# Sums of the down projection's weights made in both token blocks, with weights fetched a slice ahead, and final norms by pairs of tiles

## The chip, the cores and the metric

The kernel runs on one core of a Trainium2 chip. The metric is the device time of one execution in microseconds (us). Inside the core, TensorE (PE) multiplies; VectorE (DVE), ScalarE (ACT) and GpSimd (POOL) do the elementwise work; SyncE (SP) and POOL issue most of the DMAs. Each engine works through its own instructions strictly in order, and waits on semaphores for the others.

## What is computed

One layer of an encoder on 2048 tokens of width 1024: a token mixer, then a SwiGLU feed-forward network with an inner width of 2816, then a last RMS norm. Cut to the part that the change touches:

```python
x = x + mix                                      # the mixer's result
h = rms_norm(x, norm2[l])
gate, up = jnp.split(h @ w_ffn_in[l], 2, axis=-1)
x = x + (jax.nn.silu(gate) * up) @ w_ffn_out[l]  # w_ffn_out: 2816 x 1024
return rms_norm(x, final_norm)
```

All data is float32, and the results have to keep nearly that precision.

## The kernel before

**Products.** Every operand of a matmul is split into a high part, which TensorE multiplies at its fast rate, and a low remainder. A product is three matmuls, high by high, low by high and high by low (`mm3`, L206 to L209 of the profile). Both halves of the feed-forward network use the Strassen-Winograd scheme: seven products of sums of blocks in place of eight products of blocks.

**Stages.** The mixer works on four blocks of 512 tokens (0 to about 757 us). Then the gate stage (class `Gate`) goes over two blocks of 1024 tokens, block 0 until about 1180 us and block 1 until about 1660 us. In each it takes 22 steps j, one for each pair of 128-wide slices of the inner width; a step has seven products of 12 matmuls 128x512, so 84 matmuls. The products' results are kept (`kept`, ACT copy L895), joined by additions on DVE (L910 to L921) and activated on ACT (L911, L922). The sums of the finished slices are made by `Gate.sums` (L949 to L972) and stored to `ad`. The feed for the following step fetches its weights (`in_wgu_dram`, SP's queue), adds them (L720 to L747) and splits them into high (ACT L217) and low (DVE L218). Last comes the stage `Down`: five groups of inner slices times eight pairs of token tiles; its fifth group also has four plain products, and after it the pair's two tiles get the final norm and are stored.

**Side work in the gate stage.** `spread` takes a list of Python generators and the number of steps of each, and hangs single steps evenly between the products of steps j0 to j1. The list is planned separately for each block:
- In block 0 it holds what block 1 needs at its start: `nb.normed` (20 steps at j 3 to 10) and `nb.differences` (24 steps, from j 12 on).
- In block 1 it holds `w2_sums(k)` for the eleven slice pairs k, at j 2 to 19. A `w2_sums` fetches four raw pieces of 128x512 of `w_ffn_out` (`in_w_dram`, L223, POOL's queue) in its first step. In seven more it forms the seven sums (DVE L995 to L1008) and calls `put` for each: ACT casts the high part (L982), DVE subtracts for the low part (L983), POOL stores both to `w2c` in memory (L985). One k, `PLAIN`, has four puts without sums. In all that is 44 loads, 74 puts and 148 stores. `Down` reads the parts back from `w2c`.

**Buffers and order.** All these buffers come from two arenas, A (float32 work, tile `arena`) and R (matmul operands, tile `arena_r`), with 140 and 264 grains of 128 columns. A freed piece is given out again, and the instruction that writes it first then waits for the last one that read it, a store among them. The engines' order is made by a scheduler from the program's order, not written by hand.

**Final norm.** `finish(s, i)` (called between the products of the next pair, in `run_all`) makes the reciprocal root for one tile by `rsqrt`: 12 instructions on 128x1 data (L195 to L204), then two scalings of 128x512 (L1170) and two stores. `Down.step` adds each product's result from its PSUM bank to the accumulator on DVE (L1101); a bank can be written again only after that.

Of the kernel before, what the change touches and what calls it, by code (L numbers as in the profile page):

```python
# [37 lines left out]
A_GRAINS = 140  # L38
R_GRAINS = 264
# [115 lines left out]
def hybrid_layer_kernel(  # L155
# [37 lines left out]
    def rsqrt(dst, ss, scale, n):  # L193
# [272 lines left out]

    def run(gen, n=None):
        while n is None or n > 0:
            if next(gen, run) is run:
                return  # L470
            if n is not None:
                n -= 1
# [502 lines left out]
    def w2_sums(k):  # L975

        raw = [load(w2[k, n][:, i * T : (i + 1) * T], T, queue=nc.gpsimd) for i in range(2) for n in range(2)]
        b11, b12, b21, b22 = raw

        def put(m, b):  # L980
# [6 lines left out]

        yield
        if k == PLAIN:
            for m, b in enumerate(raw):  # L990
                put(m, b)
                yield
            return
        t1 = A.alloc(T)
        nc.vector.tensor_sub(t1.f(), b12.f(), b11.f())  # L995
        put(0, b11)
        yield
        t2 = A.alloc(T)
        nc.vector.tensor_sub(t2.f(), b22.f(), t1.f())
        put(1, t1)  # L1000
        yield
        nc.vector.tensor_sub(b12.f(), b22.f(), b12.f())
        put(4, b12)
        yield
        put(6, b22)
        yield
        t4 = A.alloc(T)
        nc.vector.tensor_sub(t4.f(), b21.f(), t2.f())  # L1008
        put(2, t2)
        yield  # L1010
        put(3, b21)
        yield
        put(5, t4)
        yield


    class Down:
# [55 lines left out]
        def step(self, at):  # L1073
# [68 lines left out]
            if last:  # L1142
                self.finish(s, 0)
# [7 lines left out]
            if last:  # L1151
                self.finish(s, 1)
# [4 lines left out]
        def squares(self, s, i, n):  # L1157

            if (s, i) not in self.ss:
                self.ss[s, i] = [small(1, "ssf") for _ in range(2)]  # L1160
            sumsq(self.ss[s, i][n], self.acc[s][i].f(2, T)[:, n, :], T)
# [166 lines left out]
```

## Time and profile before

| what | us |
|---|---|
| median of 3 runs | 2112.72 (2112.57 to 2117.39) |
| the profiled execution, its time | 2109.95 |
| its span, first to last instruction | 2107.9 |
| TensorE busy in the span | 2021.6 (96%) |
| gate stage, block 0 | about 757 to 1180 |
| gate stage, block 1; its stretch with the weights' sums | about 1180 to 1660; 1222 to 1605 |
| Down; its last group | 1660 to 2098; 1980 to 2098 |

The page gives busy time for each engine over the whole span. A view of stretches gives the same for each stage, with the count of instructions; a view of waits says which instruction of an engine stood idle, and what released it. TensorE's busy time counts a matmul from its start to its modelled end, and matmuls overlap, so that a stretch full of matmuls at half rate still reads as busy; the count of matmuls in a stretch tells it apart.

### The profile page before, as it was taken

Reading aid. Unit: us, or ns where it says so; the run is one execution under the profiler, and the core shown is the slowest. Engines: PE = TensorE matmul, PEld = TensorE weight load, DVE = VectorE, ACT = ScalarE, POOL = GpSimd, SP = SyncE. Lnnn points to the kernel's source line nnn. Section 1 sums busy time; section 2 is a strip of 40 time slices with the busy share of each in tenths; the row PEclk is TensorE's granted clock in tenths of the full one; section 3 lists DMA queues with packets and bytes.
Section 4 is the critical chain, followed back from the end, with each engine's and each line's share of the span. In section 5 each row is a group of like instructions: output and inputs, shape, how many; then the busy total and the mean of one; then the engine's idle time right before and its main releaser. Section 6 shows DMA issues by size and latency. Waiting matters only on the chain.

```text
span 2107.9 us, 26734 instructions
## 1 busy us (share of the span) xinstructions
PE 2021.6 (96%) x9520; PEld 1656.0 (79%) x9520; DVE 1346.9 (64%) x2474; ACT 885.6 (42%) x1523; POOL 202.9 (10%) x260
## 2 busy tenths in 40 slices
PE   7999999999999999999999999998999999999997
PEld 6788778878878878788888777776777788888776
DVE  6575555464655776565766876766775556565687
ACT  5655545734654553433333644443443212111232
POOL 0000000000000000000000022222221222222110
PEclk9999999999999999999999999999999999999999
DMA  4132245245424634544653766666665955755632
GB/s 170 58 129 75 99 139 197 67 152 174 156 89 141 223 128 125 169 141 140 185 170 114 221 200 220 233 235 195 223 225 177 389 157 190 241 165 165 216 127 80
DMA packets 208359, 353.22 MB, mean 168 GB/s; under 512 B 19409, under 2 KB 95458, under 8 KB 208226
## 3 DMA queue, kind: packets, MB, share of 16 engines
q1 hardware_dynamic: 190562, 292.79, 42.8%
q0 software_dynamic: 17664, 58.73, 7.9%
q8 instruction: 74, 1.21, 0.2%
q14 instruction: 59, 0.48, 0.1%
HBM read 244.49 MB, written 106.95 MB: 167 GB/s over the span
## 4 chain that ended last, share of the span: by engine, by line
PE 64%; DMA 10%; DVE 10%; issue 9%; ACT 4%; POOL 3%; SPq 0%; POOLq 0%; DVEq 0%; ACTq 0%
PE mm L207 21%; PE mm L208 20%; PE mm L209 20%; DVE arena_r L218 2%; DMA w2c<-arena 2%; POOL w2c L985 2%; DMA arena<-in_wgu_dram 2%; DMA ad<-arena 1%; ACT arena_r L217 1%; DVE arena L1101 1%; DMA arena<-in_wf_dram 1%; DVE arena L460 1%; DMA arena_r<-w2c 1%; PE mm L794 1%; DVE arena_r L1068 1%
## 5 line engine op out<-in xcount | busy, mean ns | idle before, releaser
L207 PE MATMUL mm<-arena_r 128*128 128x512 f32 (+1 forms) x2848 | 1114.0, 392 | 48.9 <-ACT arena L895 20.8
L208 PE MATMUL mm<-arena_r 128*128 128x512 f32 (+1 forms) x2848 | 1105.1, 388 | 11.1 <-DVE arena_r L218 7.0
L209 PE MATMUL mm<-arena_r 128*128 128x512 f32 (+1 forms) x2848 | 1098.9, 388 | 6.2 <-DVE arena_r L218 6.2
L207 PEld LDWEIGHTS mm<-arena_r 128*128 128x128 f32 x2848 | 538.5, 189 | 184.5 <-ACT arena L895 35.6
L217 ACT CAST arena_r<-arena 128x512 fp32r<-128x512 f32 (+1 forms) x638 | 376.8, 610 | 626.3 <-PE mm L208 299.2
L209 PEld LDWEIGHTS mm<-arena_r 128*128 128x128 f32 x2848 | 539.4, 190 | 118.0 <-DVE arena_r L218 9.1
L208 PEld LDWEIGHTS mm<-arena_r 128*128 128x128 f32 x2848 | 540.2, 190 | 116.6 <-DVE arena_r L218 14.0
L218 DVE TENSOR_TENSOR arena_r<-arena,arena_r 128x512 fp32r<-128x512 f32 (+1 forms) x638 | 411.7, 674 | 263.2 <-ACT arena_r L217 194.7
L1101 DVE TENSOR_TENSOR arena<-arena,mm 128x512 f32<-128x512 f32 x288 | 197.4, 687 | 139.0 <-PE mm L209 138.8
L1067 ACT CAST arena_r<-arena_r 128x896 fp32r<-128x896 f32 (+1 forms) x88 | 80.5, 915 | 302.4 <-PE mm L208 174.0
L1068 POOL TENSOR_TENSOR arena_r<-arena_r 128x896 fp32r<-128x896 f32 x40 | 85.0, 2125 | 323.4 <-PE mm L209 178.0
L985 POOL DMA_DIRECT2D w2c<-arena x148 | 80.1, 543 | 188.1 <-ACT arena L982 154.8
L190 ACT ACTIVATE arena<-arena 128x512 bf16<-128x512 f32 (+1 forms) x80 | 57.0, 713 | 83.8 <-DVE arena L1101 42.8
L223 POOL DMA_DIRECT2D arena<-in_w_dram x44 | 23.8, 542 | 675.1 <-DMA arena<-in_wgu_dram 573.9
L895 ACT COPY arena<-mm 128x512 f32<-128x512 f32 x132 | 76.5, 580 | 9.4 <-PE mm L209 9.4
L982 ACT CAST arena<-arena 128x512 fp32r<-128x512 f32 x74 | 45.6, 620 | 79.7 <-DMA arena<-in_w_dram 24.0
L918 DVE TENSOR_TENSOR arena<-mm,arena 128x512 f32<-128x512 f32 x44 | 30.3, 688 | 41.9 <-PE mm L209 41.9
L1068 DVE TENSOR_TENSOR arena_r<-arena_r 128x896 fp32r<-128x896 f32 (+1 forms) x48 | 50.1, 1044 | 9.8 <-ACT arena_r L1067 9.2
L983 DVE TENSOR_TENSOR arena<-arena 128x512 fp32r<-128x512 f32 x74 | 49.6, 687 | 9.2 <-ACT arena L982 8.4
L910 DVE TENSOR_TENSOR arena<-mm,arena 128x512 f32<-128x512 f32 x44 | 30.3, 688 | 39.2 <-PE mm L209 39.2
L616 POOL COPY stc<-arena 128x256 f32<-128x256 f32 x4 | 3.6, 904 | 473.6 <-ACT arena L190 134.2
L921 DVE TENSOR_TENSOR arena<-mm,arena 128x512 f32<-128x512 f32 x44 | 30.3, 689 | 28.0 <-PE mm L209 28.0
(133 smaller groups left out, 1113.7 us busy)
## 6 DMA issues: line engine op xcount, KB each, us to landing
arena<-in_wgu_dram SPq DMA_DIRECT2D x176, 256.0 KB, 3.6
ad<-arena SPq DMA_DIRECT2D x148, 256.0 KB, 3.4
w2c<-arena POOLq DMA_DIRECT2D x148, 256.0 KB, 3.7
arena_r<-w2c SPq DMA_DIRECT2D x148, 256.0 KB, 5.6
arena_r<-ad SPq DMA_DIRECT2D x80, 448.0 KB, 3.6
arena<-in_wf_dram SPq DMA_DIRECT2D x40, 512.0 KB, 3.6
arena<-in_wo_dram SPq DMA_DIRECT2D x32, 512.0 KB, 3.7
arena<-in_w_dram POOLq DMA_DIRECT2D x44, 256.0 KB, 4.4
```

The source lines that it names most:

```text
L190: nc.scalar.activation(b.ap.bitcast(BF16), src, AF.Square, accum_out=dst)
L207: nc.tensor.matmul(ps, lhsT=sh, rhs=mh, start=first, stop=False, skip_group_check=again)
L208: nc.tensor.matmul(ps, lhsT=sh, rhs=ml, start=False, stop=False, skip_group_check=again)
L209: nc.tensor.matmul(ps, lhsT=sl, rhs=mh, start=False, stop=last, skip_group_check=again)
L217: nc.scalar.copy(hi, src)
L218: nc.vector.tensor_sub(lo, src, hi.bitcast(F32))
L895: nc.scalar.copy(b.f(), ps[:, :n])
L983: nc.vector.tensor_sub(b.f().bitcast(F32R), b.f(), hi.f())
L985: nc.gpsimd.dma_start(w2c[k][:, m, i * T : (i + 1) * T], part.f())
L1067: nc.scalar.copy(hi, v)
L1068: (nc.gpsimd if i == 1 else nc.vector).tensor_tensor(lo, v, hi.bitcast(F32), op=ALU.subtract)
L1101: nc.vector.tensor_add(c, c, ps)
```

## The change

- `w2_sums` becomes one generator for all eleven k. It fetches the four raw pieces of the next k right after the fifth of seven puts of a k (for `PLAIN` after the third of four), before the last two puts. The sums themselves and `put` stay.
- This one generator is hung into both gate blocks: 30 of its 75 steps in block 0 at j 12 to 19, 45 in block 1 at j 2 to 19. To make room, `normed` moves from j 3 to 10 to j 3 to 7, and `differences` from j 12 on to j 8 to 11.
- Arena A gets 144 grains, R 260.
- `rsqrt` becomes a generator of parts. `finish` takes a pair's two tiles at once, with the 12 small instructions on 128x2 data for both, and one part of it is run before each further product of the next pair. The last pair is still done by single tiles.

```diff
-A_GRAINS = 140
-R_GRAINS = 264
+A_GRAINS = 144
+R_GRAINS = 260
...
-    def rsqrt(dst, ss, scale, n):
+    def rsqrt_parts(dst, ss, scale, n):
...
+            if it != 1:
+                yield
+
+    def rsqrt(*args):
+        run(rsqrt_parts(*args))
...
-    def w2_sums(k):
-
-        raw = [load(w2[k, n][:, i * T : (i + 1) * T], T, queue=nc.gpsimd) for i in range(2) for n in range(2)]
-        b11, b12, b21, b22 = raw
-
-        def put(m, b):
+    def w2_sums(ks):
+
+        raws = {}
+
+        def fetch(i):
+            if i < len(ks):
+                k = ks[i]
+                raws[i] = [load(w2[k, n][:, h * T : (h + 1) * T], T, queue=nc.gpsimd)
+                           for h in range(2) for n in range(2)]
+
+        def put(k, m, b):
...
+        fetch(0)
         yield
...
+            t4 = A.alloc(T)
+            nc.vector.tensor_sub(t4.f(), b21.f(), t2.f())
+            put(k, 2, t2)
+            fetch(i + 1)
+            yield
+            put(k, 3, b21)
+            yield
+            put(k, 5, t4)
+            yield
...
-        def finish(self, s, i):
-
-            rs = small(1, "rsf")
-            rsqrt(rs, self.ss.pop((s, i)), 1.0 / D, 1)
-            b, t = self.acc[s][i], self.tiles(s)[i]
...
+        def finish(self, s, which=(0, 1)):
+
+            m = len(which)
+            rs = small(m, "rsf")
+            i0 = which[0]
+            yield from rsqrt_parts(rs, [v[:, i0 : i0 + m] for v in self.ss[s]], 1.0 / D, m)
+            for i in which:
+                b, t = self.acc[s][i], self.tiles(s)[i]
+                for n in (1, 0):
...
+                    yield
+                A.free(b)
...
-                    if ks == len(self.groups) - 1 and r in (2, 4) and s > 0:
-                        self.finish(s - 1, r // 2 - 1)
+                    if r:
+                        run(done, 1)
                 run(nxt)
+                run(done)
+                if ks == len(self.groups) - 1:
+                    done = self.finish(s)
...
+    w2_side = w2_sums(range(NJ // 2))
...
-            spread([nb.normed(hf) for hf in range(2)], [KC + 2] * 2, 3, 11)
-            spread([nb.differences(c) for c in range(4)], [6] * 4, 12, NJ - 3)
+            spread([nb.normed(hf) for hf in range(2)], [KC + 2] * 2, 3, 8)
+            spread([nb.differences(c) for c in range(4)], [6] * 4, 8, 12)
+            spread([w2_side], [30], 12, NJ - 2)
         else:
-            spread([w2_sums(k) for k in range(NJ // 2)], [8] * (NJ // 2), 2, NJ - 2)
+            spread([w2_side], [45], 2, NJ - 2)
```

The changed program has as many instructions on TensorE, ACT, SP and POOL as before; on DVE it has 84 fewer. Its lines are numbered anew: L223 is L235, L982, L983 and L985 are L992, L993 and L995, L895 is L900, L217 is L229, L1101 is L1118, L1170 is L1190, and L195 to L204 are L202 to L211.

On POOL's queue, before, from the middle of the sums in block 1: `in_w_dram` is a raw weight piece that is fetched, `w2c` a part that is stored, and POOL takes no other work there.

```order
L223 DMA arena<-in_w_dram 128x512 x3
L985 DMA w2c<-arena 128x512 x13
L223 DMA arena<-in_w_dram 128x512 x2
L985 DMA w2c<-arena 128x512
L223 DMA arena<-in_w_dram 128x512 x2
L985 DMA w2c<-arena 128x512 x10
L223 DMA arena<-in_w_dram 128x512 x3
```

On POOL's queue, after, the end of block 0's part and the start of block 1's; `x2d` pieces are accumulators of `Down`'s first pairs.

```order
L235 DMA arena<-in_w_dram 128x512 x3
L995 DMA w2c<-arena 128x512 x13
L235 DMA arena<-in_w_dram 128x512 x2
L995 DMA w2c<-arena 128x512
L235 DMA arena<-in_w_dram 128x512 x2
L995 DMA w2c<-arena 128x512 x7
L235 DMA arena<-x2d_70 128x1024
L235 DMA arena<-x2d_74 128x1024
L995 DMA w2c<-arena 128x512 x3
L235 DMA arena<-in_w_dram 128x512
```

The queue's pattern stays, loads with stores between them, since a load can go only into a piece that is free; what moved is its place against the matmuls, and the two `x2d` loads, which stood ahead of all sums.

On DVE, before, the last group of `Down`, near its end: the small instructions of one tile's norm among the additions.

```order
L1101 TENSOR_TENSOR arena<-arena,mm 128x512
L202 SCALAR_TENSOR_TENSOR rt<-ry 128x1
L203 TENSOR_TENSOR rt<-rt,rv 128x1
L204 SCALAR_TENSOR_TENSOR rsf<-rt,ry 128x1
L195 TENSOR_SCALAR rv<-ssf 128x1
L1170 SCALAR_TENSOR_TENSOR arena<-arena,rsf 128x512
L1101 TENSOR_TENSOR arena<-arena,mm 128x512
L1170 SCALAR_TENSOR_TENSOR arena<-arena,rsf 128x512
L197 SCALAR_TENSOR_TENSOR rv<-ssf,rv 128x1
L199 TENSOR_SCALAR ry<-rv 128x1
L202 SCALAR_TENSOR_TENSOR rt<-ry 128x1
L203 TENSOR_TENSOR rt<-rt,rv 128x1
```

On DVE, after, at the same place, with the norm of a pair of tiles.

```order
L1118 TENSOR_TENSOR arena<-arena,mm 128x512
L210 TENSOR_TENSOR rt<-rt,rv 128x2
L211 SCALAR_TENSOR_TENSOR rsf<-rt,ry 128x2
L1190 SCALAR_TENSOR_TENSOR arena<-arena,rsf 128x512 x3
L1118 TENSOR_TENSOR arena<-arena,mm 128x512
L1190 SCALAR_TENSOR_TENSOR arena<-arena,rsf 128x512
L1118 TENSOR_TENSOR arena<-arena,mm 128x512 x5
L202 TENSOR_SCALAR rv<-ssf 128x2
L204 SCALAR_TENSOR_TENSOR rv<-ssf,rv 128x2
L206 TENSOR_SCALAR ry<-rv 128x2
L209 SCALAR_TENSOR_TENSOR rt<-ry 128x2
```

The small instructions come once for a pair, and five additions follow each other without any; three of the pair's four scalings stand together ahead of an addition.

## Rows read from the trace of the kernel before

**Rows 1.** The page: busy time, share of the span and instructions of each engine.

```profile
PE 2021.6 (96%) x9520; PEld 1656.0 (79%) x9520; DVE 1346.9 (64%) x2474; ACT 885.6 (42%) x1523; POOL 202.9 (10%) x260
```

**Rows 2.** Stretches: from:to, length, busy (count) of PE, PEld, DVE, ACT, POOL; clock, DMA share, GB/s.

```profile
757.00:1004.00 247.00, 243.11 (x1094) 198.47 (x1093) 153.20 (x252) 101.94 (x177) 0.00 (x0) 1.00 0.43 137
1004.00:1160.00 156.00, 155.90 (x683) 127.35 (x683) 103.62 (x166) 58.07 (x100) 0.00 (x0) 1.00 0.53 160
...
1222.00:1605.00 383.00, 353.57 (x1494) 282.81 (x1492) 272.74 (x436) 163.11 (x285) 101.58 (x188) 0.98 0.68 224
...
1660.00:1672.00 12.00, 8.72 (x32) 6.48 (x31) 6.72 (x8) 1.82 (x4) 3.67 (x4) 0.86 1.04 355
1672.00:1980.00 308.00, 308.00 (x1358) 254.52 (x1357) 184.02 (x257) 61.94 (x67) 68.57 (x33) 1.00 0.62 205
1980.00:2098.00 118.00, 111.56 (x475) 87.56 (x474) 95.17 (x273) 35.74 (x80) 12.75 (x6) 1.00 0.31 104
```

**Rows 3.** TensorE's waits, 1222 to 1605 us: us in total, times, longest.

```profile
PE mm L207 <- ACT arena L895: 17.3, 13, 3.8
PE mm L207 <- DVE arena L915: 7.0, 3, 3.3
```

**Rows 4.** ACT's waits for DMAs, 1222 to 1605 us.

```profile
ACT arena L982 <- DMA arena<-in_w_dram: 24.0, 9, 6.4
ACT arena L982 <- DMA w2c<-arena: 21.6, 9, 4.2
...
ACT arena L982 <- DMA ad<-arena: 8.4, 4, 3.2
```

**Rows 5.** DVE's waits for DMAs, 1222 to 1605 us.

```profile
DVE arena L995 <- DMA arena<-in_w_dram: 19.2, 6, 6.1
...
DVE arena L956 <- DMA w2c<-arena: 7.6, 5, 2.9
...
DVE arena L965 <- DMA w2c<-arena: 4.2, 2, 2.5
```

**Rows 6.** Timeline around 1507 us: start, length, instruction, idle before and its releaser.

```profile
1506.75 0.54 POOL L223 DMA_DIRECT2D arena<-in_w_dram  x1 [4.90 <-DMA w2c<-arena]
...
1510.22 0.69 DVE L995 TENSOR_TENSOR arena<-arena 128x512 f32<-128x512 f32 x1 [6.09 <-DMA arena<-in_w_dram]
1510.30 1.79 ACT L982 CAST arena<-arena 128x512 fp32r<-128x512 f32 x3 [5.07 <-DMA arena<-in_w_dram]
1510.83 0.68 DVE L915 TENSOR_TENSOR arena<-mm,arena 128x512 f32<-128x512 f32 x1
...
1511.57 0.80 PE L207 MATMUL mm<-arena_r 128*128 128x512 f32 x1 [3.28 <-DVE arena L915]
...
1512.16 0.63 PE L208 MATMUL mm<-arena_r 128*128 128x512 f32 x1
...
1512.59 0.63 PE L209 MATMUL mm<-arena_r 128*128 128x512 f32 x1
```

**Rows 7.** DMA issues, 1222 to 1605 us: KB each, median us to landing.

```profile
w2c<-arena POOLq DMA_DIRECT2D x148, 256.0 KB, 3.7
...
arena<-in_w_dram POOLq DMA_DIRECT2D x40, 256.0 KB, 4.9
```

**Rows 8.** TensorE's waits, block 0, 757 to 1160 us.

```profile
PE mm L207 <- ACT arena L895: 2.3, 3, 1.3
```

**Rows 9.** DVE by line and shape, 1980 to 2108 us: count, busy, mean ns, idle before.

```profile
L1101 DVE TENSOR_TENSOR arena<-arena,mm 128x512 f32<-128x512 f32 x59 | 40.1, 684 | 12.1 <-PE mm L209 11.9
L1170 DVE SCALAR_TENSOR_TENSOR arena<-arena,rsf 128x512 f32<-128x512 f32 x32 | 22.9, 749 | 0.3
...
L203 DVE TENSOR_TENSOR rt<-rt,rv 128x1 f32<-128x1 f32 x48 | 7.6, 158 | 1.4
```

**Rows 10.** DVE by line and shape, whole span: the small product two wide.

```profile
L203 DVE TENSOR_TENSOR rt<-rt,rv 128x2 f32<-128x2 f32 x6 | 0.9, 156 | 0.1
```

**Rows 11.** TensorE's waits, 1980 to 2098 us.

```profile
PE mm L207 <- DVE arena L1101: 6.1, 8, 1.2
```

More of the change, by code (lines that the diff above doesn't have):

```diff
@@ L191, in sumsq, with run @@
         A.free(b)
-    def rsqrt(dst, ss, scale, n):
+    def run(gen, n=None):
+        while n is None or n > 0:
+            if next(gen, run) is run:
+                return
+            if n is not None:
+                n -= 1
+    def rsqrt_parts(dst, ss, scale, n):
         v = small(n, "rv")
@@ L465, in lru_scan @@
         return mb
[L467 to L472, printed above, removed]
     class OutProj:
@@ L986, in put @@
             A.free(hi, b)
+        fetch(0)
         yield
[L989 to L1014, printed above, removed]
+        for i, k in enumerate(ks):
+            raw = raws.pop(i)
+            b11, b12, b21, b22 = raw
+            if k == PLAIN:
+                for m, b in enumerate(raw):
+                    put(k, m, b)
+                    if m == 2:
+                        fetch(i + 1)
+                    yield
+                continue
+            t1 = A.alloc(T)
+            nc.vector.tensor_sub(t1.f(), b12.f(), b11.f())
+            put(k, 0, b11)
+            yield
+            t2 = A.alloc(T)
+            nc.vector.tensor_sub(t2.f(), b22.f(), t1.f())
+            put(k, 1, t1)
+            yield
+            nc.vector.tensor_sub(b12.f(), b22.f(), b12.f())
+            put(k, 4, b12)
+            yield
+            put(k, 6, b22)
+            yield
+            t4 = A.alloc(T)
+            nc.vector.tensor_sub(t4.f(), b21.f(), t2.f())
+            put(k, 2, t2)
+            fetch(i + 1)
+            yield
+            put(k, 3, b21)
+            yield
+            put(k, 5, t4)
+            yield
     class Down:
@@ L1142, in step @@
             if last:
-                self.finish(s, 0)
+                run(self.finish(s, (0,)))
             add(c22, pd)
@@ L1151, in step @@
             if last:
[L1152 removed]
+                run(self.finish(s, (1,)))
                 for m in range(4):
@@ L1157, in squares @@
         def squares(self, s, i, n):
-            if (s, i) not in self.ss:
-                self.ss[s, i] = [small(1, "ssf") for _ in range(2)]
-            sumsq(self.ss[s, i][n], self.acc[s][i].f(2, T)[:, n, :], T)
-        def finish(self, s, i):
-            rs = small(1, "rsf")
-            rsqrt(rs, self.ss.pop((s, i)), 1.0 / D, 1)
-            b, t = self.acc[s][i], self.tiles(s)[i]
-            for n in (1, 0):
-                v = b.f(2, T)[:, n, :]
-                nc.vector.scalar_tensor_tensor(v, v, rs, self.fn.f(2, T)[:, n, :], op0=ALU.mult, op1=ALU.mult)
-                nc.sync.dma_start(out_v[t][:, n * T : (n + 1) * T], v)
-            A.free(b)
+            if s not in self.ss:
+                self.ss[s] = [small(2, "ssf") for _ in range(2)]
+            sumsq(self.ss[s][n][:, i : i + 1], self.acc[s][i].f(2, T)[:, n, :], T)
+        def finish(self, s, which=(0, 1)):
[6 more added lines that the diff above has]
+                for n in (1, 0):
+                    v = b.f(2, T)[:, n, :]
+                    nc.vector.scalar_tensor_tensor(v, v, rs[:, which.index(i) : which.index(i) + 1],
+                                                   self.fn.f(2, T)[:, n, :], op0=ALU.mult, op1=ALU.mult)
+                    nc.sync.dma_start(out_v[t][:, n * T : (n + 1) * T], v)
+                    yield
+                A.free(b)
         def run_all(self, ready):
```

## The prediction

> **What bounds the kernel now.** I read the page first: TensorE is busy for 96% of the span [rows 1], so only two things can shorten the program, fewer matmuls or fewer stretches in which matmuls come late. The change has the same matmuls. So the second view is the one of stretches, and what the reader is to see there is length against count. From 1672 to 1980 us TensorE never idles at full clock: 1358 matmuls in 308 us, 0.2268 us each [rows 2]. I take this as the full rate and ask what the other stretches lose by it. Block 1's stretch with the weights' sums has 1494 matmuls, which need 338.8 us and take 383: it loses 44 us. The last group has 475, 107.7 us, and takes 118: it loses 10. The entry to Down, 1660 to 1672 us, has 32, 7.3 us, and takes 12: it loses nearly 5. Block 0 idles for 3.9 us in its first stretch and 0.1 us in its second [rows 2]; nothing can be won there, but something lost. Behind the last matmul stand about 10 us of norms and stores (2098 to the span's end at 2107.9).
>
> In the sums' stretch the idle time alone is 383 - 353.6 = 29.4 us. The other 15 us are in the busy part: behind a wait of 3.28 us at 1511.57 matmuls start 0.43 us apart (1512.16, 1512.59) [rows 6], and the mean granted clock of the stretch is 0.98 against 1.00 [rows 2]; 0.43 is about twice 0.2268, the lower of the clock's two levels. So a long wait costs its length and some more behind it. The Trainium skill, Perfetto Trace Analysis, section Identifying the Most-Contended Engine, says that busy time of pipelined matmuls is a poor measure, and to look at the share of weight loads. That share is 282.81/383 = 0.738 here and 254.52/308 = 0.826 at full rate [rows 2], so by the rule the stretch loses 383 x (1 - 0.738/0.826) = 41 us; by idle time, 29; a forecast made in proportion to the rule's figure would lie 1 to 2 us above mine.
>
> Who makes TensorE wait there? It waits mostly for the ACT copy L895 (17.3 us) and the DVE addition L915 (7.0 us) [rows 3], the instructions that empty a PSUM bank. They are not slow. They stand in order behind an ACT cast L982 or a DVE subtraction L995 of the weights' sums, which waits for a DMA. Rows 6 show one such chain: a raw load is issued at 1506.75, after POOL had waited 4.90 us for a store to give the buffer free; DVE L995 and ACT L982 wait for its data until 1510.2 and 1510.3; L915 runs at 1510.83 right behind L995; TensorE starts at 1511.57. ACT and DVE together wait there 24.0 + 19.2 = 43.2 us for raw loads, and 21.6 + 8.4 + 7.6 + 4.2 = 41.8 us for stores that still hold a buffer, of the sums or of the gate's results [rows 4, 5].
>
> **The change part by part.** A, the weights' sums. No instruction of them is saved: 44 loads, 74 puts, 148 stores. Three things move. First, a raw load was issued in the step before its first use; now two puts earlier. By the order and its waits the gap between the point at which a load's buffer is free and its first use was 1 to 24 matmuls in the old program (18 or fewer for seven of the eleven k), that is 0.2 to 5.4 us at 0.2268, under or near the median landing of 4.9 us [rows 7]. In the new one it is 18 to 144 for all but the first k (4 to 33 us), nearly all above 4.9 us. So the waits for loads should go. Secondly, the sums go over 8 + 18 = 26 steps j in place of 18, so all waits thin out by 18/26, if they come by crowding. Thirdly, against it: casts that write a buffer out of which a store of the sums is still running, with only 11 to 13 matmuls between (2.5 to 3 us against a landing of 3.7 us [rows 7]), number 13 in place of 7, seven of them in block 0. Counted as places where a DMA stands less than 43 matmuls ahead of the product that it can hold up, there are about 16 in place of 17, now nearly all stores.
>
> The price: loads are 43.2 of 85.0 us of the DMA waits, 51%, so 44 x 0.51 = 22 us goes with them. Of the remaining 22 us, thinning would leave 22 x 18/26 = 15, and the nearly doubled close stores would push it up to about 40 (22 x 13/7); since store waits are the shorter ones (21.6/9 = 2.4 us against 19.2/6 = 3.2 us [rows 4, 5]), a slower clock follows them less often. I take 20, near the lower end, as the count of all close places is about unchanged and the worst ones are gone. A = 20 - 44 = -24 us; ends: -39 (5 us left, about the 3.9 us of block 0 [rows 2]) and +20 (rival 4).
>
> B, block 0. `normed` and `differences` are squeezed into 9 steps j; DVE then has, by the order, at most 28 instructions in one step of block 0, about what block 1 has now (436 instructions in 383 us are 24.5 per 84 matmuls; 0.63 us each, 17 us of a step's 19 [rows 2]). Their loads and stores go by SP's queue, ahead of the gate's weight loads. Block 0 now has one kind of wait worth naming, 2.3 us in three [rows 8]. I take +2, ends 0 and +5 (a further 2.3 us, twice over). What hides this work is DVE's slack: without it each instruction more would cost its 0.6 us.
>
> C, final norms. For seven of the eight pairs the 12 small instructions come once in place of twice: 84 fewer. One takes (7.6 + 1.4)/48 = 0.19 us with its gap [rows 9], and two wide 156 ns against 158 ns [rows 9, 10], so the second tile is free: 84 x 0.19 = 16 us of DVE time less in a stage in which DVE is busy 95 of 118 us [rows 2]. On the path lies what stands between two additions L1101, for which TensorE waits 6.1 us in eight waits [rows 11]; the stage loses 10. But the order bunches three scalings, 3 x 749 ns = 2.2 us, ahead of an addition, once a pair, and a pair has eleven products whose adds can lag. I take -4, ends -8 and 0. C adds no wait on ACT or POOL; the tail of 10 us keeps its single tiles.
>
> D, moved pieces. The entry to Down keeps its instructions; the two `x2d` loads now stand on POOL between the sums, behind stores that wait for ACT, and are due only in Down's first pairs, after at least 1660 us, hundreds of us later. The arenas' new sizes shift buffers in the mixer, too. I take 0 with +/-4 (about the entry's 5 us [rows 2]).
>
> Sum: -24 + 2 - 4 + 0 = -26 us on the profiled 2109.95, so 2084. The median of the runs shown is 2.8 us above the profiled time, so 2086.5 by it.
>
> **The rivals.** Rival 1, all DMA waits of the sums go: 39 us in the sums' stretch, C -6, B +2, in sum -43, so 2070; with C at its end of -8 and B at 0 it is 2066, and a part of D's 4 us makes it 2064. For it: without sums, from 1672 on, the same engines keep TensorE at full rate [rows 2]; against it: the close stores. Rival 2, the loads come late still: several k (1, 5, 7, 8, 9) have only 18 to 30 matmuls, 4 to 7 us, ahead, and POOL's queue puts a load behind stores that wait for ACT. Then half of the loads' 22 us stays: -26 + 11 = -15, so 2098. Rival 3, the change moves the wait rather than ends it: raws held longer leave fewer buffers, and puts wait for stores as long as they did for loads. For it: already now 41.8 us of waits are of this kind, and the close stores double. Then A is 0 and only C and B remain, -2 to -5: 2108 to 2111, no change that can be told. The Trainium skill, Perfetto Trace Analysis, section Optimization Strategy, says the same of consistent bubbles on the engine that should be saturated: they can mean too little on-chip memory for the next tile. The waits on stores bear it out for half of the time. Rival 4, slower: the loss comes by step j, not by put. DVE in block 0 from j 12 on has 24 instructions a step, as many as block 1 has now, and the copies that empty banks stand behind them in the same way; block 1's still has 22. A step lost 44/18 = 2.44 us; 26 such steps lose 64, +20 on A, with B and C +18: 2131. It decides from the point at which a step still loses over 44/26 = 1.7 us. Against it: rows 3 to 6 name DMAs, not DVE's own work, and block 0's second stretch runs at full rate with 20 DVE instructions a step (166 per 683 matmuls [rows 2]).
>
> **How the numbers follow.** Forecast 2086 with 0.40; rival 1 0.18; rival 2 0.20; rival 3 0.12; rival 4 0.10. The range of 8 in 10 runs from rival 1's lower end, 2064, over the forecast with its ends of B, C and D (2077 to 2098) and rival 2 to 2108, where rival 3 begins. About 0.3% (6.3 us) can be told from no change: faster is under 2106.4, slower over 2119. The first three cases are faster, 0.78; rival 3 is the same, 0.12; rival 4 slower, 0.10.
>
> **What would show it.** In the changed kernel: waits of ACT L992 and DVE L1011 for `in_w_dram` near 0 (A; rival 2 if 10 us or more stay in each); waits of ACT L992 for `w2c` about 20 us over both blocks (rival 3 if over 60); the stretch of block 1's sums, by count, losing under 15 us, and block 0 from j 12 on some 5 to 8; the last group losing about 6 (C). A loss per step in block 0 of over 2.4 us from j 12 on would make rival 4 right. The prediction is wrong above all if TensorE's waits on L900 stay in number while their releaser's cause turns from loads to stores.

## The result and the profile after

The changed kernel takes 2139.40 us (median of 4 runs, 2137.70 to 2140.22) against 2112.64: a ratio of 1.0125, interval 1.0102 to 1.0148. It is 27 us slower, where 26 us faster was forecast.

First the page and the view of stretches, cut at the places that answer to [rows 1, 2] (from:to, length, busy time and count of PE, PEld, DVE, ACT, POOL, clock, DMA share, GB/s).

```profile
PE 2023.2 (95%) x9520; PEld 1655.7 (77%) x9520; DVE 1348.5 (63%) x2390; ACT 885.6 (41%) x1523; POOL 203.2 (10%) x260
```

```profile
0.00:790.30 790.30, 729.03 (x3904) 605.88 (x3905) 457.41 (x959) 411.47 (x727) 8.43 (x16) 0.97 0.39 129
790.30:1003.00 212.70, 212.24 (x961) 173.52 (x959) 140.60 (x226) 87.37 (x148) 1.50 (x3) 1.00 0.57 177
1003.00:1182.00 179.00, 167.77 (x716) 134.05 (x715) 127.16 (x201) 74.07 (x130) 39.47 (x74) 0.99 0.63 206
...
1255.00:1625.00 370.00, 349.96 (x1489) 281.15 (x1488) 247.83 (x385) 148.53 (x258) 60.35 (x112) 0.98 0.55 178
...
1710.00:1726.00 16.00, 9.34 (x31) 7.23 (x30) 4.37 (x7) 1.88 (x2) 2.08 (x1) 0.79 0.86 329
...
2005.00:2128.00 123.00, 120.43 (x523) 97.08 (x522) 86.90 (x191) 37.25 (x81) 14.90 (x7) 1.00 0.40 135
```

And the mixer's stretch of the kernel before, which the prediction did not take up:

```profile
0.00:763.00 763.00, 729.33 (x3904) 607.04 (x3905) 454.26 (x956) 411.07 (x726) 8.85 (x18) 0.99 0.40 135
```

Read them by length against count, at 0.2268 us for a matmul. The mixer's 3904 matmuls take 790.3 us where they took 763: 27 us are lost before the first line that the change was about. Block 0's sums (1003 to 1182) have 716 matmuls, 162.4 us, and lose 16.6. Block 1's (1255 to 1625) have 1489, 337.7 us, and lose 32.3. Together that is 49 us, against 44 before: the sums' loss moved, and none of it went. The entry to Down (1710 to 1726) has 31 matmuls, 7 us, in 16: 9 lost, against 5. The last group has 523, 118.6 us, in 123: it loses 4.4, against 10. So +27 in the mixer, +5 in the sums, +4 at the entry, -6 in the last group: +30, which is what lies between the two profiled executions (2140.22 and 2109.95 us).

**The mixer.** In the view of TensorE's waits from 0 to 757 us the first line below is of the kernel before, the second of the changed one (L229 is the old L217).

```profile
PE mm L207 <- ACT arena_r L217: 3.6, 3, 2.1
```

```profile
PE mm L219 <- ACT arena_r L229: 34.8, 9, 13.9
```

Two waits make up most of the 34.8 us. The timeline of SP's queue before (a row joins issues that follow each other; the second column is the time that they take together, gaps included) and after, near the first:

```profile
60.97 0.81 SPq L223 DMA_DIRECT2D arena<-in_wf_dram  x2
82.14 21.12 SPq L223 DMA_DIRECT2D arena<-in_x_dram  x4
103.53 12.91 SPq L223 DMA_DIRECT2D arena<-in_wf_dram  x3
```

```profile
61.35 0.33 SPq L235 DMA_DIRECT2D arena<-in_wf_dram  x1
82.19 20.92 SPq L235 DMA_DIRECT2D arena<-in_x_dram  x4
103.21 11.82 SPq L235 DMA_DIRECT2D arena<-in_wf_dram  x4
...
110.96 1.14 ACT L229 CAST arena_r<-arena 128x512 fp32r<-128x512 f32 x2 [2.20 <-DMA arena<-in_wf_dram]
...
111.63 0.80 PE L219 MATMUL mm<-arena_r 128*128 128x512 f32 x1 [12.59 <-ACT arena_r L229]
```

One weight piece `in_wf` that stood ahead of four x pieces stands behind them now. Those four go into buffers that DVE still works in (in the kernel before, SP waits 14.5 us for the scan L460 alone), so SP, in order, spends 21 us on them; the weight piece starts at 103.2, ACT casts it at 110.96, and TensorE has nothing to multiply for 12.59 us. Near 440 us a piece of `in_wo` that stood ahead of two of seven x pieces stands behind all seven; before (SP's queue) and after:

```profile
424.15 5.18 SPq L223 DMA_DIRECT2D arena<-in_x_dram  x5
429.61 0.33 SPq L223 DMA_DIRECT2D arena<-in_wo_dram  x1
```

```profile
422.56 20.67 SPq L235 DMA_DIRECT2D arena<-in_x_dram  x7
446.46 1.41 SPq L235 DMA_DIRECT2D arena<-in_wo_dram  x2
...
452.42 1.14 ACT L229 CAST arena_r<-arena 128x512 fp32r<-128x512 f32 x2 [4.91 <-DMA arena<-in_wo_dram]
...
453.08 0.79 PE L219 MATMUL mm<-arena_r 128*128 128x512 f32 x1 [13.94 <-ACT arena_r L229]
```

Here the order is not all of it. The last x piece is out by 443.2 us, and SP's own waits from 443.3 to 446.6 us show that the weight piece then waits until DVE's subtraction has left the buffer that it goes into:

```profile
SPq L235 <- DVE arena_r L230: 3.2, 1, 3.2
```

The kernel before waits at these two places as well, 3.9 and 4.1 us. By the starts of the same matmuls in both kernels the first place costs 10.9 us more than before and the second 8.6; the rest of the 27 us comes in shorter pieces.

**The sums.** The waits of ACT and DVE for DMAs, in block 0's stretch of sums and then in block 1's (L992 is the cast, L1011 the first sum; these answer to [rows 4, 5]).

```profile
ACT arena L992 <- DMA w2c<-arena: 10.8, 6, 2.2
...
ACT arena L992 <- DMA ad<-arena: 4.4, 2, 3.7
...
ACT arena L992 <- DMA arena<-in_w_dram: 2.9, 2, 1.7
```

```profile
DVE arena L1011 <- DMA arena<-in_w_dram: 5.6, 2, 5.0
```

```profile
ACT arena L992 <- DMA w2c<-arena: 26.9, 11, 5.0
```

```profile
DVE arena L1011 <- DMA w2c<-arena: 8.5, 2, 4.4
...
DVE arena L1011 <- DMA arena<-in_w_dram: 0.5, 1, 0.5
```

TensorE's waits in the same two stretches (these answer to [rows 8, 3]; L900 is the old L895):

```profile
PE mm L219 <- ACT arena L900: 5.3, 5, 1.8
```

```profile
PE mm L219 <- ACT arena L900: 11.4, 6, 4.2
```

The fetch ahead did what it says: waits for raw loads fell from 43.2 us to 2.9 + 5.6 + 0.5 = 9.0. But the cast's waits for stores of the sums rose from 21.6 us to 10.8 + 26.9 = 37.7, and `L1011`, which waited for loads, waits 8.5 us for stores. The matmuls wait as before, for the same copies: 5.3 + 11.4 = 16.7 us in 11 waits, against 17.3 us in 13 where the sums ran before. One more wait grew: DVE's for the gate's own weight loads (`in_wgu_dram`, L725, the old L720) was 10.9 us from 940 to 1630 us before and is 21.8 us now.

### The profile page after: what moved, and what is told of

The parts are those of the page before. It is cut to its first block, busy times and chain, and to the rows that moved or that the text cites. A ratio compares the mean times of both kernels' runs of the same rounds, so it can differ in the third digit from the quotient of the medians.

```text
span 2138.4 us, 26620 instructions
## 1 busy us (share of the span) xinstructions
PE 2023.2 (95%) x9520; PEld 1655.7 (77%) x9520; DVE 1348.5 (63%) x2390; ACT 885.6 (41%) x1523; POOL 203.2 (10%) x260
## 4 chain that ended last, share of the span: by engine, by line
PE 65%; DMA 11%; issue 10%; DVE 8%; ACT 4%; POOL 1%; SPq 0%; DVEq 0%; POOLq 0%; ACTq 0%
PE mm L219 21%; PE mm L221 21%; PE mm L220 21%; DVE arena_r L230 2%; DMA w2c<-arena 2%; DMA ad<-arena 2%; DMA arena<-in_wo_dram 1%; POOL w2c L995 1%; ACT arena_r L229 1%; DMA arena<-in_wgu_dram 1%; DMA arena<-in_x_dram 1%; DMA arena<-in_wf_dram 1%; DMA arena_r<-ad 1%; PE mm L799 1%; DMA arena<-in_wg_dram 1%
## 5 line engine op out<-in xcount | busy, mean ns | idle before, releaser
L229 ACT CAST arena_r<-arena 128x512 fp32r<-128x512 f32 (+1 forms) x638 | 377.1, 610 | 628.5 <-PE mm L220 297.0
L230 DVE TENSOR_TENSOR arena_r<-arena,arena_r 128x512 fp32r<-128x512 f32 (+1 forms) x638 | 420.3, 674 | 288.3 <-ACT arena_r L229 243.3
L1118 DVE TENSOR_TENSOR arena<-arena,mm 128x512 f32<-128x512 f32 x288 | 197.2, 686 | 151.3 <-PE mm L221 151.3
L995 POOL DMA_DIRECT2D w2c<-arena x148 | 79.8, 541 | 406.1 <-ACT arena L992 339.3
L992 ACT CAST arena<-arena 128x512 fp32r<-128x512 f32 x74 | 45.5, 620 | 97.5 <-DMA w2c<-arena 37.7
L900 ACT COPY arena<-mm 128x512 f32<-128x512 f32 x132 | 76.6, 580 | 14.7 <-PE mm L221 14.6
L993 DVE TENSOR_TENSOR arena<-arena 128x512 fp32r<-128x512 f32 x74 | 50.5, 690 | 27.4 <-ACT arena L992 25.8
L235 POOL DMA_DIRECT2D arena<-in_w_dram x44 | 23.7, 540 | 406.8 <-DMA ad<-arena 353.2
L923 DVE TENSOR_TENSOR arena<-mm,arena 128x512 f32<-128x512 f32 x44 | 30.3, 688 | 44.5 <-PE mm L221 44.3
L725 DVE TENSOR_TENSOR arena<-arena 128x512 f32<-128x512 f32 x44 | 30.3, 689 | 31.1 <-DMA arena<-in_wgu_dram 23.9
L915 DVE TENSOR_TENSOR arena<-mm,arena 128x512 f32<-128x512 f32 x44 | 30.2, 687 | 22.1 <-PE mm L221 22.1
```

The lines of the kernel that those rows point to most:

```text
L229: nc.scalar.copy(hi, src)
L230: nc.vector.tensor_sub(lo, src, hi.bitcast(F32))
L900: nc.scalar.copy(b.f(), ps[:, :n])
L993: nc.vector.tensor_sub(b.f().bitcast(F32R), b.f(), hi.f())
L995: nc.gpsimd.dma_start(w2c[k][:, m, i * T : (i + 1) * T], part.f())
L1118: nc.vector.tensor_add(c, c, ps)
```

## The experiments

Below, "loss" is the time from one matmul's start to another's, by their ordinal in the timeline, less 0.2268 us for each: for block 0 the 4913th to the 5725th (from j 12 on), for block 1 the 5950th to the 7480th (j 2 to 19). "Mixer" is the time from the first to the 3905th. Each comes from one profiled execution, and executions of one kernel differ (the kernel before took 2104.99 to 2121.25 us on one chip); the ratios come from the timed runs, against the kernel before on the same chip.

| kernel | median us | ratio (interval) | mixer | loss, block 0 | loss, block 1 |
|---|---|---|---|---|---|
| before | 2112.64 | 1 | 753.3 | 1.5 | 44.9 |
| the change | 2139.40 | 1.0125 (1.0102 to 1.0148) | 780.5 | 17.2 | 34.9 |
| arenas_alone | 2128.14 | 1.0063 (1.0041 to 1.0086) | 781.1 | 2.3 | 43.6 |
| after_old_arenas | 2115.98 | 1.0016 (0.9994 to 1.0037) | 753.8 | 21.5 | 31.2 |
| arenas_142_262 | 2092.24 | 0.9908 (0.9884 to 0.9932) | 756.7 | 2.3 | 28.5 |
| arenas_143_261 | 2112.15 | 1.0008 (0.9987 to 1.0029) | 773.8 | 1.6 | 34.0 |
| change_142_262 | 2099.05 | 0.9941 (0.9924 to 0.9959) | 758.8 | 9.3 | 17.9 |
| ahead_block1 | 2109.90 | 0.9975 (0.9957 to 0.9993) | 755.4 | 1.3 | 51.6 |
| spread_no_ahead | 2110.04 | 0.9989 (0.9966 to 1.0013) | 752.0 | 14.4 | 30.6 |
| finish_alone | 2109.70 | 0.9989 (0.9970 to 1.0008) | 755.1 | 1.3 | 45.1 |
| stores_elsewhere | 2109.89 | 0.9991 (0.9973 to 1.0009) | 786.8 | 1.7 | 10.0 |
| no_casts | 2094.18 | 0.9913 (0.9890 to 0.9937) | 756.8 | 1.3 | 30.7 |
| pool_sums | 2110.41 | 0.9986 (0.9974 to 0.9999) | 758.0 | 22.4 | 29.2 |
| open_part_spread_ahead | 2086.11 | 0.9880 (0.9853 to 0.9907) | 752.7 | 13.5 | 14.6 |
| open_part_spread | 2081.56 | 0.9857 (0.9834 to 0.9880) | 754.0 | 14.6 | 12.5 |
| open_part_block1_ahead | 2103.76 | 0.9961 (0.9940 to 0.9982) | 752.1 | 2.3 | 43.7 |
| open_part_block1 | 2113.67 | 1.0019 (1.0002 to 1.0037) | 752.9 | 2.6 | 57.9 |
| open_part_spread_b | 2105.92 | 0.9964 (0.9947 to 0.9981) | 753.4 | 15.3 | 28.2 |
| open_part_spread_ahead_b | 2099.96 | 0.9949 (0.9928 to 0.9969) | 753.4 | 15.7 | 27.7 |
| open_part_block1_b | 2103.58 | 0.9961 (0.9945 to 0.9978) | 753.0 | 1.9 | 48.4 |

### The arenas' sizes and the mixer

**arenas_alone**, on the kernel before:

```diff
-A_GRAINS = 140
-R_GRAINS = 264
+A_GRAINS = 144
+R_GRAINS = 260
```

> The kernel before with only the arenas' sizes of the change (A 144, R 260 grains). Theory 1, the sizes: the mixer's 22 to 24 us that the changed kernel is late by at its end come from where buffers now lie, so this kernel is about 24 us slower than before (2137), with two waits of TensorE of 12 to 14 us for ACT casts near 111 and 453 us. Theory 2, the rest of the change moves the mixer's order too: this kernel is within 5 us of before.

Two constants make the mixer 28 us longer in the profile, with the two waits at their places, of 12.60 and 14.03 us:

```profile
111.40 0.79 PE L207 MATMUL mm<-arena_r 128*128 128x512 f32 x1 [12.60 <-ACT arena_r L217]
...
454.68 0.80 PE L207 MATMUL mm<-arena_r 128*128 128x512 f32 x1 [14.03 <-ACT arena_r L217]
```

Theory 1 holds: the sizes cause the mixer's loss, not the moved side work. The timed runs are slower by 13 us (1.0063), less than the 24 expected; the rest of the program moved too, its last group losing 5 us where before lost 10.

**after_old_arenas**, the other way round: the change with 140 and 264 grains.

> The changed kernel with the arenas of before (140, 264). Theory 1: the mixer returns to before's time, and the time is 2139 - 24 = 2115 or, if the smaller A costs the sums more waits for stores, up to 2122. Theory 2: it stays near 2139.

The mixer is back (753.8 us), and the time is 2115.98, no different from before that can be told. Taken out of the change the sizes give back 23 us; put into the kernel before they cost 13. So the sizes are about half of the change's 27 us or more, and how much depends on what else is in the program. Without them its sums lose 52.7 us, 6 more than before.

**arenas_142_262**, half the step, on the kernel before:

> The kernel before with arenas of 142 and 262 grains, half of the change's step. In SP's queue the mixer's first weight loads then stand as before (three in_wf pieces ahead of the second set of four x pieces, not two). If the mixer's loss in arenas_alone comes from that piece's place behind the x loads, this kernel is within 4 us of before, and the 12.6 us wait near 110 us is not there. If every shift of the arenas costs the mixer, it is 8 us or more slower.

The mixer is 3.4 us longer than before, without the 12.6 us wait; its `in_wf` pieces stand in SP's queue as before. Not expected was the gain: block 1's sums lose 28.5 us, 16 less than before, though no instruction of theirs changed. Only the places of buffers did.

**arenas_143_261**, one grain more:

> The kernel before with one grain more for arena A than arenas_142_262 (143 and 261). From this size on, SP's queue has one in_wf piece fewer ahead of the second set of x pieces. If that order is what the change lost 22 us by, the mixer is 18 us or more longer than in arenas_142_262, with a wait near 110 us of 10 us or more. If the loss needs the full step of the sizes or comes from elsewhere, the mixer is within 5 us of before.

The first wait is there, and TensorE stands for 12.82 us:

```profile
61.24 0.33 SPq L223 DMA_DIRECT2D arena<-in_wf_dram  x1
82.08 20.92 SPq L223 DMA_DIRECT2D arena<-in_x_dram  x4
103.11 12.02 SPq L223 DMA_DIRECT2D arena<-in_wf_dram  x4
...
111.76 0.80 PE L207 MATMUL mm<-arena_r 128*128 128x512 f32 x1 [12.82 <-ACT arena_r L217]
```

The mixer is 17.1 us longer than with 142 grains, near the 18 expected; 10 us of it come at this wait. The second wait, that near 454 us, does not come with this size: its `in_wo` piece still stands ahead of two x pieces. So one grain, 128 columns, turns the place of one load, and that costs a wait of 12.8 us; the second piece turns between 143 and 144.

**change_142_262**, the change with 142 and 262 grains:

> The change whole, with arenas of 142 and 262 grains in place of 144 and 260, so that the mixer's order of loads stays as before. If arenas' sizes are the whole cause of its 27 us of slowdown: 2110 to 2118, a mixer within 5 us of before and 45 to 55 us of loss in the sums. If the change is slow by the sums themselves: 2125 or more.

It beats the kernel before by 0.6%, and the change as made by 40 us, by two constants; the kernel before with the same sizes (arenas_142_262, 0.9908) is still ahead of it (0.9941). The mixer takes 758.8 us, 5.5 more than before and 21.7 less than in the change. The rest of the difference is placing again: the sums lose 27.2 us in place of 52.1, under the 45 to 55 expected, while block 0 ahead of them (j 0 to 11) takes 237.3 us where the change takes 223.9.

### The sums

**ahead_block1**: the fetch ahead and the new norms, with the arenas of before and all sums in block 1.

```diff
...
-            spread([w2_side], [30], 12, NJ - 2)
...
         else:
-            spread([w2_side], [45], 2, NJ - 2)
+            spread([w2_side], [75], 2, NJ - 2)
```

> Arenas of before, new final norms, the fetch ahead, but all 75 steps of the weights' sums in block 1 as before (normed and differences at their old places). If the waits for loads cost 22 us and nothing takes their place: 2112.7 - 22 - 3 = 2088. If waits for stores take their place (rival 3): 2106 to 2112, block 1's stretch losing 40 us or more.

2109.90 and a loss of 51.6 us: the fetch ahead alone takes nothing off block 1's loss. From 940 to 1630 us the waits for raw loads are down to 6.8 us, all on DVE, where ACT and DVE had 43.2; and ACT's waits for stores of the sums, 21.6 us in nine before, are now

```profile
ACT arena L992 <- DMA w2c<-arena: 54.6, 28, 6.5
```

So the wait moved from loads to stores, at the old arenas and the old places of the sums: rival 3's description.

**spread_no_ahead**: over both blocks, but each k fetched in the step before its use (34 steps in block 0, 51 in block 1), with the new norms and the arenas of before.

```diff
         for i, k in enumerate(ks):
+            fetch(i)
+            yield
             raw = raws.pop(i)
...
```

> Arenas of before, new final norms, the sums over both blocks, but each k's raw weights fetched in the step before their first use, as before. If crowding decides, thinning to 26 of 18 steps leaves 44 x 18/26 = 30 us of loss: 2112.7 - 14 - 3 = 2096. If the loss goes by put, not by step (74 puts either way): 2108 to 2112, with about 18 us of loss in block 0 and 27 in block 1.

14.4 + 30.6 = 45 us of loss, as much as before: spread over 26 steps, the loss did not thin. It is as if it went by put (45/74 = 0.6 us each), not by step. This is one placing of the buffers, though, and the expected gain of 14 us is no larger than what placing alone does (16 us in arenas_142_262).

**stores_elsewhere**, on the kernel before; its stores leave out the sums' parts and copy a raw piece from memory to memory:

```diff
-                nc.gpsimd.dma_start(w2c[k][:, m, i * T : (i + 1) * T], part.f())
+                nc.gpsimd.dma_start(w2c[k][:, m, i * T : (i + 1) * T], w2[k, i][:, :T])
```

> The kernel before, but each of the 148 stores of the sums copies a raw weight piece of the same size from memory to w2c instead of the buffer that was made, so the numbers of the down projection are not the reference's; all casts, subtractions, sums and bytes stay, only no buffer waits for a store and no store for a cast. Theory of buffers (waits move from loads to stores because buffers are short): most of block 1's 45 us of loss goes, 2075 to 2085. Theory of crowding (each put's own work on ACT and DVE delays the instructions that empty banks): the loss stays above 30 us, 2100 to 2110.

The total did not move, and lies where the theory of crowding put it; the stages tell otherwise. Block 1's stretch, with all of its DVE and ACT instructions, and TensorE's waits from 940 to 1650 us:

```profile
1254.00:1611.00 357.00, 352.10 (x1533) 287.00 (x1532) 277.88 (x444) 167.93 (x291) 21.41 (x40) 1.00 0.43 132
```

```profile
PE mm L207 <- ACT arena L895: 5.1, 4, 2.2
```

Its loss is 10 us in place of 45, with 444 instructions on DVE and 291 on ACT (436 and 285 in [rows 2]). So the elementwise work in itself does not cost the 45 us; what hangs on the stores does. But the copies, waiting for nothing any more, all ran in the mixer (issued from 2.4 to 160.4 us), and the mixer became 33.5 us longer:

```profile
w2c<-in_w_dram POOLq DMA_DIRECT2D x148, 256.0 KB, 8.2
```

Thus the run can't part a store's hold on its buffer from its bytes and its place ahead of the loads on POOL's queue.

**no_casts**, on the kernel before: no cast, no subtraction, no buffer for the high part.

```diff
-            hi = A.alloc(T)
-            nc.scalar.copy(hi.f().bitcast(F32R), b.f())
-            nc.vector.tensor_sub(b.f().bitcast(F32R), b.f(), hi.f())
-            for i, part in enumerate((hi, b)):
+            for i, part in enumerate((b, b)):
...
```

> The kernel before, but a put stores the sum twice and leaves out the ACT cast and the DVE subtraction (74 each) and the buffer for the high part, so the down projection's numbers are not the reference's; loads, sums, stores and bytes stay. Theory of crowding, or of ACT as the engine that is held up: the 17 us of waits for the ACT copy go and the loss falls under 25 us, 2090 or less. Theory of the DMAs alone (loads, DVE's sums waiting for them): the loss stays above 30 us.

The time falls by 0.9%, block 1's loss to 30.7 us, between the two theories: just above the 30 us that the second names, and 14 under before. In TensorE's waits (940 to 1650 us) the ACT copy mostly leaves, 4.0 us for 18.8, and the split's subtraction comes, 10.8 us for 2.3:

```profile
PE mm L209 <- DVE arena_r L218: 10.8, 4, 4.4
PE mm L207 <- DVE arena L915: 5.0, 2, 2.8
PE mm L207 <- ACT arena L895: 4.0, 3, 2.0
```

The edit takes away a buffer for each put along with the cast, so the run does not part ACT's work from the buffers.

**pool_sums**: after_old_arenas with all elementwise work of the sums on POOL.

```diff
-            nc.scalar.copy(hi.f().bitcast(F32R), b.f())
-            nc.vector.tensor_sub(b.f().bitcast(F32R), b.f(), hi.f())
+            nc.gpsimd.tensor_copy(hi.f().bitcast(F32R), b.f())
+            nc.gpsimd.tensor_sub(b.f().bitcast(F32R), b.f(), hi.f())
...
-            nc.vector.tensor_sub(t1.f(), b12.f(), b11.f())
+            nc.gpsimd.tensor_sub(t1.f(), b12.f(), b11.f())
...
```

> The changed kernel with the arenas of before, and all elementwise work of the weights' sums (74 casts, 74 subtractions, 60 sums) on POOL instead of ACT and DVE. If the loss comes from ACT and DVE standing in order behind that work and its DMA waits, about 45 of the 52 us of loss in both blocks go: 2065 to 2075. Against it: POOL takes about 1.2 us for each (2125 ns for 896 columns in the trace of before), 250 us in all besides 104 us of issuing, so the sums may end late and hold up the first loads of Down: 2090 to 2120.

No gain: 51.6 us of loss. POOL's subtraction takes 1460 ns, and while POOL works DVE's own are slower (the last section). At TensorE's longest wait in this stage, 7.32 us until 1028.34, the copy L900 stands on ACT behind a cast that waits for DVE, and DVE takes 4.75 us for two subtractions that take 0.69 us each in the kernel before:

```profile
1017.43 4.75 DVE L230 TENSOR_TENSOR arena_r<-arena,arena_r 128x512 fp32r<-128x512 f32 x2
...
1025.10 0.62 ACT L229 CAST arena_r<-arena 128x512 fp32r<-128x512 f32 x1 [9.69 <-DVE arena L730]
```

So the edit puts a new delay in place of the old one, and the run does not show whether the sums' order on ACT and DVE was what cost the time.

### More of the arena opened

The allocator takes the lower 48 of arena A's grains only when no other place is free. The open_part kernels open them in the gate stage; the "b" kernels use other limits, and so place every buffer anew. open_part_block1_ahead has limits of its own, too (open until j 18, and pieces freed less than 36 frees ago taken last, where open_part_block1 has j 13 and 12 frees), so these two differ by more than the fetch ahead.

```diff
             gens = [blk.gate_up(j) for j in js]
+            A.border = 0 if (bi and js[0] < 14) or (not bi and 2 <= js[0] < 20) else A_BORDER
...
```

> The changed kernel with the arenas of before, and in the gate stage (block 0 from j 2, block 1 until j 13) the lower 48 grains of arena A opened to all buffers, which the allocator else takes last; so a freed piece rests longer before it is written again. Theory of buffers (a piece is written again while its store runs): of the 52 us of loss in both blocks' sums about half goes, 2085 to 2095. Theory of traffic (the bytes of loads and stores make the loads of the gate late): no gain, 2110 to 2118.

> As spread_no_ahead (sums over both blocks, no fetch ahead, arenas of before), with the lower grains of arena A opened as in open_part_spread_ahead. Theory of buffers: 45 us of loss fall to 15 to 25, 2080 to 2090. If the fetch ahead matters once buffers are free, open_part_spread_ahead is the faster one by 5 us or more; else they are alike.

> As ahead_block1 (all sums in block 1, fetch ahead, arenas of before), with the lower grains of arena A opened until j 18 of block 1, and pieces freed less than 36 frees ago (12 before) taken last. Theory of buffers: the 51 us of loss fall to 15 to 25, 2075 to 2085, since by the order fewest close reuses are left here. Theory of traffic: 2105 to 2112.

> The kernel before with the new final norms and the lower grains of arena A opened in the gate stage as in open_part_spread; sums as before, all in block 1, no fetch ahead. With before, spread_no_ahead and open_part_spread this makes a square of two causes. If the thinning over two blocks is worth nothing by itself and the buffers everything: the loss of the sums falls from 45 to 27 us, 2090. If both are needed at once: 40 us or more stay, 2102 to 2110.

The first two came out as the theory of buffers has it: 28.1 and 27.1 us of loss against 52.7 and 45.0 with the grains closed. In open_part_spread the stretch of block 1 that holds the sums is nearly full (the first line is block 0's part):

```profile
975.00:1160.00 185.00, 175.73 (x752) 142.35 (x752) 132.22 (x213) 78.04 (x136) 39.39 (x73) 0.98 0.64 209
1222.00:1600.00 378.00, 371.29 (x1613) 301.97 (x1613) 259.40 (x413) 159.08 (x276) 61.91 (x115) 1.00 0.57 182
```

Its 2081.56 us are the best of all, 1.4% under before. With all sums in block 1 open grains bring nothing that the theory of buffers named (43.7 and 57.9 us of loss there, against 51.6 and 45.1 closed; the 2103.76 us of the first lie near the 2105 to 2112 of the theory of traffic). That looked like two causes needed at once, so three corners were run with another placing.

> As open_part_spread, with another placing of the buffers: the lower grains are open until j 16 of block 1, and pieces freed less than 24 frees ago (12 before) are taken last. If the gain of open_part_spread comes from spreading and open grains together: again 24 to 35 us of loss in both blocks' sums, 2080 to 2092. If it was one lucky placing: 40 us or more, 2097 to 2110.

> The same second placing for open_part_spread_ahead (with the fetch ahead). If the cause is general: 24 to 35 us of loss, 2082 to 2095; if placing alone decides: 40 us or more. The fetch ahead is worth something if this is under open_part_spread_b by 5 us or more.

> Another placing for open_part_block1 (all sums in block 1, lower grains open until j 13, 36 frees in place of 12). If density in block 1 is what keeps the loss there, whatever the placing: 40 us or more of loss, 2100 to 2115. If open_part_block1's 57 us were bad luck of its placing: 20 to 30 us, 2085 to 2092.

The spread kernels now lose 43.5 and 43.4 us. So 16 us lie between two placings of the same edit, nearly as much as the gain was, and two single corners would not have shown a cause. What stays: with open grains the four spread kernels lose 27 to 44 us and the three with all in block 1 lose 46 to 61. The gap speaks for spreading where buffers are free, but is no larger than what placing does. The fetch ahead makes no difference that can be told when the sums are spread (28.1 against 27.1, 43.4 against 43.5).

### The final norms

**finish_alone**: the kernel before with only the new norms.

> The kernel before with only the final norms by pairs of tiles. Prediction's step C: 4 us faster (2109), the last group losing 5 to 6 us by count instead of 10. Rival: the three scalings that stand together ahead of an addition cost what the small instructions cost, and the time stays within 1 us of before.

By the timed runs there is no difference that can be told (interval 0.9970 to 1.0008). In the profiles the last group (9060th to 9510th matmul) loses 7.0 us here and 10.0 to 10.3 in the three kernels with arenas of 140 grains and the old norms: 3 us gained. With 144 grains it loses 5.1 us with the old norms and 4.8 with the new: nothing.

## Why the prediction was wrong

**The step that failed: D.** "The arenas' new sizes shift buffers in the mixer, too. I take 0 with +/-4." It was +27 in the profile's mixer, and arenas_alone shows that the sizes alone do it (+28 there, 13 us in the timed runs). The bound came from the size of another wait (the entry's 5 us), not from the order: in SP's queue of the two programs one weight piece has changed sides of four x pieces, and the trace of before shows that SP spends 21 us on those four. That could be read from what was there. (D also held the entry to Down, below.) Without it the change would have been near where rival 3 stood, no change that can be told (after_old_arenas, 2115.98).

**A failed, too, in size and sign.** The waits for raw loads went as forecast, from 43.2 to 9.0 us. But A = -24 took for granted that their half of the loss would go with them. It came back as waits for stores, 37.7 us for ACT's cast in place of 21.6, and A is +5. At equal arenas the sums with and without the change lose 52.7 and 46.4 us (140 grains), 27.2 and 30.8 (142), 52.1 and 45.9 (144), and the ratios are 1.0016 and 1, 0.9941 and 0.9908, 1.0125 and 1.0063: at none of the three sizes did A come near -24, and at none did the change gain time. What the prediction named as the sign of being wrong above all is what came: TensorE's waits on L900 stay in number (11 for 13) while their cause turns from loads to stores. The prediction had the count that speaks for this (close stores 13 in place of 7) and weighed it as rival 3 with 0.12. Rival 3's named sign was over 60 us of waits of ACT for `w2c`, and it was 38; its mechanism holds all the same, by ahead_block1, which fetches ahead, waits 54.6 us for those stores and loses 51.6 us. The thinning by 18/26 did not come in spread_no_ahead, as far as one placing can say.

**Rival 4** had the sign of the result but not its cause: a step of block 0 from j 12 on loses 17.2 us over 9.7 steps, 1.8 us each, which is over the 1.7 from which that rival decides and under its 2.44; but the crowding by DVE's work falls by stores_elsewhere, where the same work loses 10 us.

**B** was near nothing here: block 0 to j 11 takes 223.9 us for 225.8. It is no constant, though: with other arenas the same edit takes 230.6 us (spread_no_ahead), 232.1 (after_old_arenas) and 237.3 (change_142_262). **C**, -4, was -5 in this profile, but with these arenas the old norms do as well; its own effect is 3 us at the old sizes, and the timed runs can't tell it from nothing. **The entry to Down**, part of D's +/-4, lost 4 more than before: a late load of the gate's sums holds ACT's split, and behind it the additions.

```profile
1715.15 0.94 ACT L1084 CAST arena_r<-arena_r 128x896 fp32r<-128x896 f32 x1 [12.39 <-DMA arena_r<-ad]
...
1717.92 0.80 PE L219 MATMUL mm<-arena_r 128*128 128x512 f32 x1 [6.66 <-DVE arena L1118]
```

**What stays open:** what in the stores costs the time (the held buffer, the bytes, for which the longer waits for the gate's own loads speak without showing it, or POOL's order; stores_elsewhere removed all of them together), and how much spreading is worth, since the same code lost 28 to 45 us in block 1 by arena sizes alone. The prediction's last sum should read 2086.7 in place of 2086.5, which changes nothing.

## What to carry to other kernels

A constant that sets where buffers lie is a change of the whole program: compare the order of every queue, in the stages that the change doesn't speak of first, and price a load that changes sides by what the queue spends on the ones that it now follows. Taking away one of two waits that end on the same instruction gains only what the other leaves; look for what is late next before taking a share of the loss. Where an allocator's placing alone moves a stage by 15 us, one kernel with and one without an edit show nothing below that: vary the placing on both sides.

## What the runs showed of the hardware

Work on POOL slows DVE's. In pool_sums, from 1255 to 1625 us, DVE's split subtraction takes 983 ns where it takes 686 in the same stage of before, with the same shape (line, names, shapes, count, busy time, mean ns, idle before). The first row is of before; the second and third are of pool_sums, the third an addition that reads one input from PSUM; the last two are POOL's own instructions in the whole span of pool_sums.

```profile
L218 DVE TENSOR_TENSOR arena_r<-arena,arena_r 128x512 fp32r<-128x512 f32 x125 | 81.4, 686 | 12.3 <-PE mm L209 5.6 <-ACT arena_r L217 3.7 <-PE mm L208 2.6
```

```profile
L230 DVE TENSOR_TENSOR arena_r<-arena,arena_r 128x512 fp32r<-128x512 f32 x126 | 119.1, 983 | 32.4 <-PE mm L221 28.2 <-PE mm L220 4.1
...
L915 DVE TENSOR_TENSOR arena<-mm,arena 128x512 f32<-128x512 f32 x18 | 12.4, 688 | 12.6 <-PE mm L221 12.5
```

```profile
L993 POOL TENSOR_TENSOR arena<-arena 128x512 fp32r<-128x512 f32 x74 | 108.0, 1460 | 3.9
...
L992 POOL CAST arena<-arena 128x512 fp32r<-128x512 f32 x74 | 59.7, 810 | 96.4 <-DVE arena L928 34.7 <-DMA w2c<-arena 27.1 <-DVE arena_r L230 16.4
```

The Trainium skill, SBUF — State Buffer, section SBUF: two separate sides, says that a DVE instruction with two inputs in SBUF and a GpSimd instruction that reads SBUF take one pair of ports in turn, each for its whole length. The rows agree: 297 ns more on the average for a DVE subtraction, next to POOL instructions of 810 to 1460 ns, while the addition with one input in PSUM stays at 688 ns.

A copy of 256 KB from memory to memory, 148 of them in a row, took 8.2 us at the median from issue to landing, against 3.7 us for the stores of the same size out of a buffer [rows 7], and made the mixer beside them 33.5 us longer.
